# One-megabyte modulation units through GpSimd's queue, and recurrence results parked in DRAM, in a two-layer diffusion backbone

## The chip, the cores and the metric

The program runs on one core of a Trainium2 chip. The metric is the device time of one execution in microseconds (us); lower is better. A core has five engines with instruction streams of their own: TensorE (PE, matmuls), VectorE (DVE), ScalarE (ACT), GpSimd (POOL) and SyncE (SP, which here only issues transfers). Each engine takes its instructions strictly in order and waits on semaphores for the others. Transfers are issued from the streams of SP, ACT and POOL and run on 16 shared DMA engines.

## The reference

One inference step through two layers over 128 context and 256 latent tokens (384 columns in all) of width 2048. What matters here is the modulation (a linear map of the conditioning vectors, for each layer 2048 x 6144 weights, used as shift, scale and gate) and the first layer, where a recurrence and a Fourier mixer run as parallel head groups, each with a gate:

```python
m = (jax.nn.silu(cond) @ w + b)[..., None, :]      # modulation, split into shift, scale, gate
...
hp = _rmsnorm(xp, norm_pre[layer]) * (1.0 + sc_p) + sh_p
...
proj = h @ w_in
...
o, s_fin = _wkv_scan(...)                          # recurrence over the tokens, 16 heads of 64
o = ((o - mean) * lax.rsqrt(var + GN_EPS)).reshape(bsz, t_len, A_WIDTH)
o = o * gn_w.astype(f32) + gn_b.astype(f32)
y_a = (o + bonus.reshape(bsz, t_len, A_WIDTH)) * jax.nn.silu(gate_a)
y_b = y_b * jax.nn.silu(gate_b)
y = jnp.concatenate([y_a, y_b], axis=-1).astype(h.dtype) @ w_out
...
xp = xp + g_p * _rmsnorm(yp, norm_post[layer])
```

The second layer is grouped windowed attention with the same kind of modulation.

## The kernel before

**Weights.** All projections stream through `Stream` (L206): a raw tile of 256 KB (`raw<-we`, later `weo`, `wo`, `woo`) is loaded by SP (L236), ACT rounds it to a high part `whi` (L260), DVE subtracts to get `wlo` (L261), and PE forms three products for each block of activations (`mm3`), accumulating in `acc` (L404). In the recurrence the raw tiles have two buffers (`RAWB = 2`).

**Modulation.** The modulation weights are cut into blocks of 512 columns, and each block into four units of 1 MB (512 of the 2048 rows each, laid out as 128 partitions of 2048 numbers). The blocks are computed in four places. The blocks of layer 0's shift and scale run on PE in the head (`layer0_in`, tiles `mraw`, seven buffers). The blocks of `FILL_MODS` run on PE inside the recurrence (`fill_lane`, tile `rawf`). `PE_MODS` run on PE and `DVE_MODS` on DVE later, through `Stream` (tile `raw`). On PE, `mod_unit` multiplies a unit by the conditioning vectors in four matmuls that stand side by side in the array and accumulate in `ps_mod`. A trace shows each of these as two records, L406 for the first of a group and L410 for the rest. After a block's fourth unit ACT copies the sums to a row tile (`mrow`, L331), PE transposes it piece by piece (`ps_mt`), and DVE adds the bias (L338).

**The fill.** In the recurrence a unit is loaded in halves of 256 columns: 7 blocks x 2 halves x 4 = 56 loads of 512 KB into one buffer, each issued by SP as soon as the matmuls of the half before are done:

```python
raw = kp.tile([128, 4, 256], F32, name="rawf", tag="rawf", bufs=1)
w = self.mod_w(layer, b, u).rearrange("p (k c) -> p k c", k=4)
nc.sync.dma_start(raw, w[:, :, c0:c0 + 256])
```

**The recurrence.** Eight pairs of heads (j = 0 to 7) go through lanes that `weave` interleaves: the shifted projections (`proj_lane`), elementwise work (`wkv_elem`, with `ya`, the bonus term, at L1013), triangular systems (`wkv_lower`, and `wkv_solve` for two pairs together, whose long row of small DVE steps is L1118 and L1120), scores (`wkv_score`), the chain over chunks (`wkv_chain`) and the group norm (`wkv_norm`), which adds the normed output to `ya` (L1290). The `ya` tiles of all eight pairs (eight buffers) stay in SBUF until their gates are multiplied in (`make_y`, L540), after the recurrence and the Fourier part. GpSimd only clears small tiles here (`p` at L965, `SV` at L1172).

**What sets the order.** `weave` picks, by estimates written into the lanes, which lane emits its next piece, and so gives each instruction a priority. The fill lane's estimate for a piece is `FILL_PACE`. A list scheduler then sets the order on each engine by these priorities and by its own model of when operands are ready. Each engine, and each engine's queue of transfers, keeps that order at run time: a transfer that has to wait for its buffer holds up what stands behind it in the stream of its engine.

Of the kernel before, what the change touches and what calls it, by code (L numbers as in the profile page):

```python
# [11 lines left out]
F32 = mybir.dt.float32  # L12
# [10 lines left out]
T = TP + TS  # L23
# [4 lines left out]


FILL_MODS = [(0, 8), (0, 9), (0, 10), (0, 11), (1, 0), (1, 4), (1, 1)]  # L30
FILL_PACE = 5
PE_MODS = [(1, 5), (1, 2)]
DVE_MODS = [(1, 6), (1, 3), (1, 7)], [(1, 8), (1, 9), (1, 10), (1, 11)]

# [271 lines left out]
class K:  # L306
# [5 lines left out]
    def mod_unit(self, raw, layer, b, u, dst, c0=0):  # L312

        nc = self.nc
        key = layer, b, c0
        n = raw.shape[1] // 4
        if u == 0:  # L320
            self.macc[key] = self.pw.tile([128, 512], F32, name="ps_mod", tag="pw")
        acc = self.macc[key]
        with self.together():
            for i in range(4):
                kt = 4 * u + i
                self.mm(acc[32 * i:32 * i + 32, :n], self.silu[:, 2 * kt:2 * kt + 32], raw[:, n * i:n * i + n],
                                 start=(u == 0), stop=(u == 3), skip_group_check=True)
        if u < 3:
            return
        rows = self.mpool.tile([128, n], F32, name="mrow", tag="junk", bufs=1)  # L330
        nc.scalar.copy(rows, acc[:, :n])  # L331
        ps = self.pw.tile([128, 512], F32, name="ps_mt", tag="pw")
        m0, nm = c0 // 128, n // 128
        with self.together():
            for m in range(nm):
                self.mm(ps[:, 2 * m:2 * m + 2], rows[:, 128 * m:128 * m + 128], self.sel, start=True, stop=True)
        m1 = 48 * layer + 4 * b + m0
        nc.vector.tensor_tensor(dst[:, m0:m0 + nm], ps[:, 0:2 * nm].rearrange("p (m c) -> p m c", c=2),  # L338
                                self.modb[:, m1:m1 + nm].unsqueeze(2).to_broadcast([128, nm, 2]), op=ALU.add)
        del self.macc[key]  # L340
# [218 lines left out]
    def build(self):  # L559
# [4 lines left out]
        with ExitStack() as ctx:  # L564
            self.pw = ctx.enter_context(tc.tile_pool(name="pw", bufs=5, space=PSUM))
            self.pa = ctx.enter_context(tc.tile_pool(name="pa", bufs=3, space=PSUM))
            self.dp = ctx.enter_context(tc.tile_pool(name="dp", bufs=1, space=bass.MemoryType.DRAM))
            cp = self.cp = self.open("cp")
            self.rawp = self.open("wp")
            self.hp = self.open("hp")  # L570

            cm = cp.tile([128, 384], F32, name="cmat")
            nc.scalar.dma_start(cm, A["cmat"])
            self.ident, self.bd, self.mask = cm[:, 0:128], cm[:, 128:256], cm[:, 256:384]
            self.par_t = cp.tile([128, NPAR], F32, name="par")
            nc.scalar.dma_start(self.par_t, A["par"])

            cc = self.par_t[:, 0:32]
            th = cp.tile([128, 32], F32, name="cth")
            self.sel32 = cp.tile([128, 32], F32, name="sel")  # L580
            nc.scalar.dma_start(self.sel32, A["csel"])
            self.sel = self.sel32[:, 0:2]
            self.modb = cp.tile([128, 96], F32, name="modb")
            nc.scalar.dma_start(self.modb, A["modbc"])
            self.mcols = cp.tile([128, 16, 4, 2], F32, name="mcols")
            nc.scalar.activation(th, cc, AF.Tanh, scale=0.5)
            nc.vector.tensor_scalar(th, th, 0.5, 0.5, op0=ALU.mult, op1=ALU.add)
            self.silu = cp.tile([128, 64], F32, name="silu")
            nc.vector.memset(self.silu[:, 32:64], 0.0)
            nc.vector.tensor_tensor(self.silu[:, 0:32].rearrange("p (k c) -> p k c", c=2), th.rearrange("p (c k) -> p k c", c=2),  # L590
                                    cc.rearrange("p (c k) -> p k c", c=2), op=ALU.mult)
            eps = cp.tile([128, 3], F32, name="eps")
            nc.vector.memset(eps[:, 0:1], RMS_EPS)
            nc.vector.memset(eps[:, 1:2], GN_EPS)
            nc.vector.memset(eps[:, 2:3], 15 * math.log(2.0))
            self.eps = eps

            self.x1d = self.dp.tile([128, 3, D], F32, name="x1d")
            self.gd = self.dp.tile([2, 2, D], F32, name="gd")

            self.sd = self.dp.tile([4, 2, 128, 4], F32, name="sd")
            sq = th.rearrange("p (q c k) -> p q c k", q=4, c=2)
            nc.vector.tensor_copy(sq, self.silu[:, 0:32].rearrange("p (q k c) -> p q c k", q=4, c=2))
            nc.scalar.dma_start(self.sd.rearrange("q c p k -> p q c k"), sq)
            self.macc = {}
            self.ws = Stream(self, self.plan())
            ys = self.layer0_mix()
            acts = self.out_proj(0, ys)
            ys = self.layer1_mix(acts)
            self.out_proj(1, ys)  # L610
            for name in ("dpm", "yg", "gp", "yq", "cp"):
                self.close(name)
# [61 lines left out]
    def layer0_mix(self):  # L674
# [111 lines left out]

        def fill_lane():

            self.mpool = kp
            jobs = [(layer, b, self.mod_dst(layer, b), c0, u) for layer, b in FILL_MODS for c0 in (0, 256) for u in range(4)]  # L790

            def load(layer, b, dst, c0, u):
                raw = kp.tile([128, 4, 256], F32, name="rawf", tag="rawf", bufs=1)
                w = self.mod_w(layer, b, u).rearrange("p (k c) -> p k c", k=4)
                nc.sync.dma_start(raw, w[:, :, c0:c0 + 256])
                return raw.rearrange("p k c -> p (k c)")

            raw = load(*jobs[0])
            for n, (layer, b, dst, c0, u) in enumerate(jobs):
                yield 0.5, 0, FILL_PACE  # L800
                self.mod_unit(raw, layer, b, u, dst, c0)
                if n + 1 < len(jobs):
                    raw = load(*jobs[n + 1])

        self.weave(main_lane(), score_lane(), chain_lane(0), chain_lane(1), norm_lane(), elem_lane((0, 2, 3, 4, 5, 6, 7)), elem_lane((1,)), proj_lane(), fill_lane(),
                   lead=LEAD)
        self.close("kp")
        y = [st["y"] for st in sts]
        self.rawp = self.mpool = self.daccp = self.open("dpm", "right")
        self.srow = self.mpool.tile([128, 2, 512], F32, name="srow")  # L810
        for q in range(4):
# [7 lines left out]
            return self.yp.tile([128, T], F32, name=nm, tag="yt", bufs=self.YB)  # L819

        ys = [None] * 16
        fp = self.open("fp")
        ch = fp.tile([128, 321], F32, name="dft")
        nc.sync.dma_start(ch, A["cdft"])
# [5 lines left out]
        for g in range(4):  # L830
# [2 lines left out]
                    ys[2 * g + m] = self.make_y(fp, accs[m], y[2 * g + m])  # L833

            self.run(self.proj_cm(256, acts, ga_done))
        self.close("fp")
        self.close("bk")
        self.close("yp0")
        self.close("hp")
# [92 lines left out]
    def wkv_elem(self, j, st):  # L932
# [75 lines left out]
        STT(sq, sq, self.hrk[:, j:j + 1], r, op0=ALU.mult, op1=ALU.mult)  # L1008
        ps = self.pw.tile([128, 512], F32, name="ps_b", tag="pw")
        self.mm(ps[:, :T], self.bd, sq, start=True, stop=True)  # L1010
        y = st["y"] = self.yp0.tile([128, T], F32, name="ya", tag="ya", bufs=8)
        yield 0, 0.67, 0
        TT(y, ps[:, :T], v, op=ALU.mult)  # L1013

# [256 lines left out]
    def wkv_norm(self, j, st):  # L1271
# [16 lines left out]
        TT(o, o, s2, op=ALU.mult)  # L1288
        ACT(o, o, AF.Identity, scale=self.par("gw", j), bias=self.par("gb", j))
        TT(y, y, o, op=ALU.add)  # L1290


    def out_proj(self, layer, ys):
# [293 lines left out]
```

## Time and profile before

| | |
|---|---|
| runs before, us | 1600.28, 1600.47, 1605.43; median 1600.47 |
| profiled execution, us | 1596.4 |
| its span, first to last instruction, us | 1594.6 |
| PE busy in the span | 95% |
| mean granted TensorE clock, as a share of full speed | 0.984 |

The profiled execution is one run of its own: 1.8 us of its 1596.4 lie outside the span. By stage, in us from the start of the span: the head to about 130, the recurrence to about 705, the Fourier part and the gates to about 860, layer 0's output projection to about 1000, attention to about 1320, and the last gates with the output projection to the end. Busy times overlap, so that they say what an engine did, not what a stage waited for; the idle time before an instruction and what ended it says that.

### The profile page before, as it was taken

How to read it: one execution, taken by the hardware profiler on the slowest of the kernel's cores; microseconds unless marked ns; L12 is line 12 of the kernel's file. 1: busy time of each engine (PE TensorE's matmuls, PEld its weight loads, DVE VectorE, ACT ScalarE, POOL GpSimd, SP SyncE). 2: the span in 40 equal slices, each digit the busy share in tenths (PEclk: the TensorE clock that was granted, in tenths of full speed). 3: DMA queues.
4: the chain of work that ended last, by engine and by line, in shares of the span. 5: the costliest groups of instructions: out<-in, count | busy, mean ns of one | idle time of the engine just before them, and what ended most of it. 6: DMA issues, size and time to landing. Idle time of an engine off the chain costs nothing.

```text
span 1594.6 us, 30005 instructions
## 1 busy us (share of the span) xinstructions
PE 1507.3 (95%) x11488; PEld 1275.6 (80%) x11488; DVE 1069.1 (67%) x2584; ACT 810.9 (51%) x1771; POOL 3.9 (0%) x21
## 2 busy tenths in 40 slices
PE   7789999989998999999999998999999999999997
PEld 2557778767776778879998778988888889998777
DVE  1426896687777685574665755899878999653344
ACT  3326756857656655454333335744556555343332
POOL 0000000000000000000000000000000000000000
PEclk9899999999999999999999999899999999999999
DMA  9985352354333243444558664565322444447443
GB/s 365 375 311 164 123 160 78 102 167 122 97 107 110 86 143 90 132 152 126 174 189 325 211 207 144 200 225 204 100 73 73 133 132 140 125 122 242 125 120 139
DMA packets 120246, 255.74 MB, mean 160 GB/s; under 512 B 12324, under 2 KB 45220, under 8 KB 109732
## 3 DMA queue, kind: packets, MB, share of 16 engines
q1 hardware_dynamic: 111528, 235.97, 44.8%
q10 hardware_dynamic: 8576, 17.86, 3.2%
q8 instruction: 90, 1.47, 0.4%
q14 instruction: 52, 0.43, 0.1%
HBM read 246.40 MB, written 7.39 MB: 159 GB/s over the span
## 4 chain that ended last, share of the span: by engine, by line
PE 64%; DVE 16%; DMA 11%; ACT 6%; issue 3%; ACTq 0%; DVEq 0%; SPq 0%
PE acc L404 31%; PE acct L404 16%; DMA rawf<-modw 5%; DVE wlo L261 3%; PE ps_mod L406 3%; DVE junk L350 2%; DMA raw<-we 2%; DMA mraw<-modw 1%; DMA raw<-modw 1%; PE ps_o L410 1%; PE ps_v L410 1%; PE ps_pv L410 1%; ACT whi L260 1%; PE ps_s L410 1%; PE ps_sa L410 1%
## 5 line engine op out<-in xcount | busy, mean ns | idle before, releaser
L260 ACT CAST whi<-raw 128x512 fp32r<-128x512 f32 x480 | 295.5, 621 | 444.7 <-PE acc L404 196.5
L261 DVE TENSOR_TENSOR wlo<-raw,whi 128x512 fp32r<-128x512 f32 x480 | 327.5, 688 | 275.6 <-ACT whi L260 270.8
L404 PE MATMUL acc<-hhi,whi 128*128 128x384 f32 x1376 | 478.3, 348 | 12.5 <-ACT whi L260 5.7
L404 PE MATMUL acc<-hlo,whi 128*128 128x384 f32 x1376 | 472.9, 344 | 0.0
L404 PE MATMUL acc<-hhi,wlo 128*128 128x384 f32 x1376 | 470.7, 343 | 1.7 <-DVE wlo L261 1.3
L404 PEld LDWEIGHTS acc<-hhi,whi 128*128 128x128 f32 x1376 | 261.3, 190 | 44.2 <-issue 18.1
L404 PEld LDWEIGHTS acc<-hlo,whi 128*128 128x128 f32 x1376 | 261.3, 190 | 13.7 <-issue 11.9
L404 PEld LDWEIGHTS acc<-hhi,wlo 128*128 128x128 f32 x1376 | 260.9, 190 | 11.1 <-issue 5.5
L350 DVE SCALAR_TENSOR_TENSOR junk<-raw,srow 128x512 f32<-128x512 f32 x224 | 154.1, 688 | 8.6 <-DMA raw<-modw 5.2
L404 PE MATMUL acct<-whi,yhi 128*128 128x512 f32 (+1 forms) x432 | 154.4, 358 | 2.4 <-DVE yb L1318 2.1
L404 PE MATMUL acct<-wlo,yhi 128*128 128x512 f32 (+1 forms) x432 | 153.9, 356 | 0.0
L404 PE MATMUL acct<-whi,ylo 128*128 128x512 f32 (+1 forms) x432 | 153.7, 356 | 0.0
L404 PEld LDWEIGHTS acct<-whi,yhi 128*128 128x128 f32 x432 | 81.5, 189 | 20.7 <-DVE yb L1318 6.5
L404 PEld LDWEIGHTS acct<-whi,ylo 128*128 128x128 f32 x432 | 81.5, 189 | 12.4 <-issue 0.2
L404 PEld LDWEIGHTS acct<-wlo,yhi 128*128 128x128 f32 x432 | 81.5, 189 | 11.8
L406 PE MATMUL ps_mod<-rawf,silu 128*32 128x256 f32 x112 | 35.0, 395 | 22.5 <-DMA rawf<-modw 22.3
L406 PE MATMUL ps_mod<-mraw,silu 128*32 128x512 f32 x64 | 35.5, 668 | 9.7 <-DMA mraw<-modw 9.7
L1118 DVE TENSOR_TENSOR work<-work 128x30 f32<-128x30 f32 (+14 forms) x120 | 39.2, 327 | 2.1
L1120 DVE TENSOR_TENSOR work<-work 128x30 f32<-128x30 f32 (+14 forms) x120 | 39.2, 327 | 1.9
L1538 DVE TENSOR_REDUCE ast<-ps_sa 128x1 f32<-128x384 f32 x64 | 25.3, 415 | 20.3 <-PE ps_sa L410 20.1
L406 PEld LDWEIGHTS ps_mod<-rawf,silu 128*32 128x32 f32 x112 | 7.7, 108 | 36.2 <-DMA rawf<-modw 25.6
L410 PE MATMUL ps_mod<-rawf,silu 128*32 128x256 f32 x336 | 35.9, 395 | 0.0
(331 smaller groups left out, 2286.5 us busy)
## 6 DMA issues: line engine op xcount, KB each, us to landing
raw<-we SPq DMA_DIRECT2D x200, 256.0 KB, 2.9
raw<-wo SPq DMA_DIRECT2D x160, 256.0 KB, 2.7
raw<-modw SPq DMA_DIRECT2D x36, 1024.0 KB, 5.2
mraw<-modw SPq DMA_DIRECT2D x32, 1024.0 KB, 8.9
rawf<-modw SPq DMA_DIRECT2D x56, 512.0 KB, 3.9
raw<-weo SPq DMA_DIRECT2D x64, 256.0 KB, 2.9
raw<-woo SPq DMA_DIRECT2D x64, 256.0 KB, 2.7
G<-gd ACTq DMA_DIRECT2D x4, 1024.0 KB, 7.4
```

The lines of the kernel that those rows point to most:

```text
L260: k.nc.scalar.copy(hi, raw)
L261: k.nc.vector.tensor_tensor(lo, raw, hi, op=ALU.subtract)
L350: nc.vector.scalar_tensor_tensor(junk, raw[:, 512 * i:512 * i + 512], 1.0, self.srow[:, c], op0=ALU.mult, op1=ALU.mult, accum_out=self.dac ...
L404: op(*args, **kw)
L406: self.head.append(op(*args, **kw).ins)
L410: op(*args, **kw)
L1118: TT(tv, X[:, s + 1:32, s:s + 1].to_broadcast([128, n, s]), X[:, s:s + 1, 0:s].to_broadcast([128, n, s]), op=ALU.mult)
L1120: TT(X[:, s + 1:32, 0:s], X[:, s + 1:32, 0:s], tv, op=ALU.add)
L1538: nc.vector.tensor_reduce(st[:, 0, i:i + 1], src[i], axis=AX.X, op=ALU.max)
```

## The change

`fill_lane` loads whole units: 28 loads of 1 MB into one buffer `rawf` of twice the size, issued from GpSimd's stream, and `FILL_PACE` is doubled. `mod_unit` no longer has a row tile; the sums of a block are copied into the beginning of the raw tile of its last unit, whose buffer is then free only when the transposes have read it. This holds for all blocks that PE computes. The `ya` tiles have five buffers in place of eight: `wkv_norm` stores each finished result to DRAM (`yd`) from ACT's stream, and after the recurrence four buffers in a new pool `yl` bring them back through GpSimd's stream, four at once and two each after the first two gate blocks.

```diff
-FILL_PACE = 5
+FILL_PACE = 10
...
-        rows = self.mpool.tile([128, n], F32, name="mrow", tag="junk", bufs=1)
+        rows = raw[:, :n]
         nc.scalar.copy(rows, acc[:, :n])
...
+            self.yd = self.dp.tile([8, 128, T], F32, name="yd")
...
-            jobs = [(layer, b, self.mod_dst(layer, b), c0, u) for layer, b in FILL_MODS for c0 in (0, 256) for u in range(4)]
-
-            def load(layer, b, dst, c0, u):
-                raw = kp.tile([128, 4, 256], F32, name="rawf", tag="rawf", bufs=1)
-                w = self.mod_w(layer, b, u).rearrange("p (k c) -> p k c", k=4)
-                nc.sync.dma_start(raw, w[:, :, c0:c0 + 256])
-                return raw.rearrange("p k c -> p (k c)")
+            jobs = [(layer, b, u, self.mod_dst(layer, b)) for layer, b in FILL_MODS for u in range(4)]
+
+            def load(layer, b, u, dst):
+                raw = kp.tile([128, 2048], F32, name="rawf", tag="rawf", bufs=1)
+                nc.gpsimd.dma_start(raw, self.mod_w(layer, b, u))
+                return raw
...
-                yield 0.5, 0, FILL_PACE
-                self.mod_unit(raw, layer, b, u, dst, c0)
+                yield 1.0, 0, FILL_PACE
+                self.mod_unit(raw, *job)
...
+        yl = self.open("yl")
+        y = [None] * 8
+
+        def y_load(j):
+            y[j] = yl.tile([128, T], F32, name="y", tag="y", bufs=4)
+            nc.gpsimd.dma_start(y[j], self.yd[j])
+
+        for j in range(4):
+            y_load(j)
...
             self.run(self.proj_cm(256, acts, ga_done))
+            if g < 2:
+                y_load(2 * g + 4)
+                y_load(2 * g + 5)
...
-        y = st["y"] = self.yp0.tile([128, T], F32, name="ya", tag="ya", bufs=8)
+        y = st["y"] = self.yp0.tile([128, T], F32, name="ya", tag="ya", bufs=5)
...
         TT(y, y, o, op=ALU.add)
+        nc.scalar.dma_start(self.yd[j], y)
```

SP's stream early in the recurrence. Before (`raw` are projection weights, `rawf` the fill's halves):

```order
L795 DMA rawf_1191<-modw 128x4x256
L236 DMA raw_1105<-we 128x512
L236 DMA raw_1123<-we 128x512
L236 DMA raw_1146<-we 128x512
L795 DMA rawf_1310<-modw 128x4x256
L236 DMA raw_1164<-we 128x512
L236 DMA raw_1197<-we 128x512
L236 DMA raw_1223<-we 128x512
L236 DMA raw_1248<-we 128x512
L236 DMA raw_1266<-we 128x512
L795 DMA rawf_1341<-modw 128x4x256
L236 DMA raw_1347<-we 128x512
```

and with the change, from the end of the head to the end of the recurrence:

```order
L629 DMA mraw<-modw 128x2048
L236 DMA raw<-we 128x512 x120
L831 DMA dft<-cdft 128x321
L833 DMA dt<-cdt 128x646
L236 DMA raw<-modw 128x2048
```

The fill's loads have left SP, whose stream through the recurrence is now 120 weight loads in a row.

GpSimd's stream with the change, in the middle of the recurrence (`p` and `SV` are its memsets, which stood there alone before; `rawf_2966` is the load of unit 13, counted from 0):

```order
L794 DMA rawf_1947<-modw 128x2048
L794 DMA rawf_2070<-modw 128x2048
L794 DMA rawf_2281<-modw 128x2048
L976 MEMSET p_2741 128x12
L794 DMA rawf_2549<-modw 128x2048
L794 DMA rawf_2712<-modw 128x2048
L1183 MEMSET SV_3676 64x2x128
L1183 MEMSET SV_3678 64x2x128
L976 MEMSET p_3369 128x12
L794 DMA rawf_2966<-modw 128x2048
L794 DMA rawf_3020<-modw 128x2048
L794 DMA rawf_3123<-modw 128x2048
```

All 28 loads stand in GpSimd's stream between these memsets, and the eight `y<-yd` loads behind the last of them.

PE's stream at a place where two units of the fill follow closely, in the scores of a pair of heads (`ps_ba` is the triangular system, `ps_sc` the scores, `ps_bt` transposes). Before:

```order
L406 MATMUL ps_ba<-AR,BK 64x64
L410 MATMUL ps_ba<-AR,BK 64x64 x7
L406 MATMUL ps_sc<-AR,BK 128x128
L410 MATMUL ps_sc<-AR,BK 128x128 x7
L406 MATMUL ps_bt<-cmat,BK 128x128
L410 MATMUL ps_bt<-cmat,BK 128x128 x3
L406 MATMUL ps_bt<-cmat,BK 128x128
L410 MATMUL ps_bt<-cmat,BK 128x128
L406 MATMUL ps_mod<-rawf,silu 32x256
L410 MATMUL ps_mod<-rawf,silu 32x256 x3
L406 MATMUL ps_bt<-cmat,BK 128x128
L410 MATMUL ps_bt<-cmat,BK 128x128 x3
```

and with the change:

```order
L406 MATMUL ps_mod<-rawf,silu 32x512
L410 MATMUL ps_mod<-rawf,silu 32x512 x3
L406 MATMUL ps_ba<-AR,BK 64x64
L410 MATMUL ps_ba<-AR,BK 64x64 x15
L406 MATMUL ps_ba<-AR,BK 64x64
L410 MATMUL ps_ba<-AR,BK 64x64 x7
L406 MATMUL ps_sc<-AR,BK 128x128
L410 MATMUL ps_sc<-AR,BK 128x128 x7
L406 MATMUL ps_sc<-AR,BK 128x128
L410 MATMUL ps_sc<-AR,BK 128x128 x7
L406 MATMUL ps_mod<-rawf,silu 32x512
L410 MATMUL ps_mod<-rawf,silu 32x512 x3
```

A group of four matmuls now covers 512 columns, there are 28 groups in place of 56, and between the two shown here stand 24 `ps_ba` and 16 `ps_sc` matmuls. The work in between is otherwise that of before: in both programs 1728 projection matmuls stand ahead of the Fourier part's first.

## Rows read from the trace of the kernel before

**Rows 1.** The page's first lines: span, then busy time of each engine.
```profile
span 1594.6 us, 30005 instructions
PE 1507.3 (95%) x11488; PEld 1275.6 (80%) x11488; DVE 1069.1 (67%) x2584; ACT 810.9 (51%) x1771; POOL 3.9 (0%) x21
```
**Rows 2.** Stages: stretch, length, busy us of each engine, granted clock, DMA share, GB/s.
```profile
0.00:130.00 130.00, 105.44 (x580) 63.43 (x581) 38.50 (x77) 42.47 (x80) 1.29 (x9) 0.95 0.84 328
130.00:605.00 475.00, 441.68 (x4764) 356.81 (x4763) 362.73 (x911) 312.94 (x663) 2.57 (x12) 0.99 0.40 123
605.00:705.00 100.00, 95.16 (x1057) 83.84 (x1055) 58.72 (x135) 52.95 (x116) 0.00 (x0) 1.00 0.45 141
```
**Rows 3.** PE's waits from 130 to 605 us: us in total, times, longest.
```profile
PE ps_mod L406 <- DMA rawf<-modw: 22.3, 20, 4.8
PE ps_bt L406 <- DVE SC L1081: 2.3, 2, 2.0
```
**Rows 4.** PE in order of time, 422 to 427 us: start, us, instruction [idle before].
```profile
422.14 0.40 PE L406 MATMUL ps_mod<-rawf,silu 128*32 128x256 f32 x1 [0.41 <-DMA rawf<-modw]
...
422.71 0.44 PE L404 MATMUL acc<-hhi,whi 128*128 128x384 f32 x1
422.99 0.34 PE L404 MATMUL acc<-hlo,whi 128*128 128x384 f32 x1
423.16 0.35 PE L404 MATMUL acc<-hhi,wlo 128*128 128x384 f32 x1
...
426.13 0.34 PE L404 MATMUL acc<-hlo,whi 128*128 128x384 f32 x1
426.96 0.40 PE L406 MATMUL ps_mod<-rawf,silu 128*32 128x256 f32 x1 [0.49 <-DMA rawf<-modw]
```
**Rows 5.** The chain of waits at the same place: start, us, transfer.
```profile
422.84 4.08 DMA rawf<-modw
```
**Rows 6.** The tile `rawf`: count, ns min/median/max, first and last start.
```profile
L406 PE MATMUL ps_mod<-rawf,silu x112: 376/379/636, 135.9 to 600.8; 128*32 128x256 f32 x112
```
**Rows 7.** PE and SP in order of time, 480 to 492 us.
```profile
481.07 0.40 PE L406 MATMUL ps_mod<-rawf,silu 128*32 128x256 f32 x1
482.33 2.46 SPq L236 DMA_DIRECT2D raw<-we  x2
484.88 0.56 SPq L795 DMA_DIRECT2D rawf<-modw  x1
490.32 0.64 PE L406 MATMUL ps_mod<-rawf,silu 128*32 128x256 f32 x1 [4.77 <-DMA rawf<-modw]
```
**Rows 8.** PE at 771 us: a unit of 512 columns in a later stage.
```profile
771.28 0.34 PE L404 MATMUL acc<-hhi,wlo 128*128 128x384 f32 x1
771.55 0.62 PE L406 MATMUL ps_mod<-raw,silu 128*32 128x512 f32 x1
772.54 0.44 PE L404 MATMUL acc<-hhi,whi 128*128 128x384 f32 x1
772.82 0.34 PE L404 MATMUL acc<-hlo,whi 128*128 128x384 f32 x1
```
**Rows 9.** The page's transfers: count, KB each, median us from issue to landing.
```profile
raw<-modw SPq DMA_DIRECT2D x36, 1024.0 KB, 5.2
mraw<-modw SPq DMA_DIRECT2D x32, 1024.0 KB, 8.9
rawf<-modw SPq DMA_DIRECT2D x56, 512.0 KB, 3.9
```
**Rows 10.** PE from 319 to 321 us: first `ps_ba`, first `ps_sc` matmul.
```profile
319.64 0.27 PE L406 MATMUL ps_ba<-AR,BK 64*64 64x64 f32 x1
320.72 0.37 PE L406 MATMUL ps_sc<-AR,BK 64*128 64x128 f32 x1
```
**Rows 11.** DVE's copies from SBUF to SBUF, 130 to 605 us: busy us, mean ns.
```profile
L1253 DVE COPY work<-SV 64x256 f32<-64x256 f32 x12 | 3.5, 292 | 0.4
L1195 DVE COPY work<-SV 64x512 f32<-64x512 f32 x6 | 2.5, 425 | 8.7 <-ACT SV L1190 8.7
L1253 DVE COPY work<-SV 64x512 f32<-64x512 f32 x6 | 2.5, 424 | 2.9 <-ACT SV L1190 2.4 <-PE ps_o L410 0.6
```
**Rows 12.** GpSimd's waits in the whole span.
```profile
POOL p L965 <- DVE BK L1021: 200.7, 5, 67.7
```
**Rows 13.** DVE in order of time: pair 0's norm, then pair 5's `ya`.
```profile
311.24 0.55 DVE L1290 TENSOR_TENSOR ya<-ya,o 128x384 f32<-128x384 f32 x1
429.20 0.56 DVE L1013 TENSOR_TENSOR ya<-ps_b,v 128x384 f32<-128x384 f32 x1 [0.43 <-PE ps_b L404]
```
**Rows 14.** The tile `gth`: the gates' readings of `ya`.
```profile
L540 DVE SCALAR_TENSOR_TENSOR gth<-gth,ya x8: 551/551/554, 790.9 to 847.6; 128x384 f32<-128x384 f32 x8
```
**Rows 15.** The tile `SV`: a store that ACT issues in the recurrence.
```profile
L1244 ACTq DMA_DIRECT2D o_st<-SV x8: 564/598/628, 270.0 to 650.7; - x8
```

More of the change, by code (lines that the diff above doesn't have):

```diff
@@ L787, in fill_lane @@
         def fill_lane():
-            self.mpool = kp
-            jobs = [(layer, b, self.mod_dst(layer, b), c0, u) for layer, b in FILL_MODS for c0 in (0, 256) for u in range(4)]
-            def load(layer, b, dst, c0, u):
-                raw = kp.tile([128, 4, 256], F32, name="rawf", tag="rawf", bufs=1)
-                w = self.mod_w(layer, b, u).rearrange("p (k c) -> p k c", k=4)
-                nc.sync.dma_start(raw, w[:, :, c0:c0 + 256])
-                return raw.rearrange("p k c -> p (k c)")
+            jobs = [(layer, b, u, self.mod_dst(layer, b)) for layer, b in FILL_MODS for u in range(4)]
[3 more added lines that the diff above has]
+                return raw
             raw = load(*jobs[0])
-            for n, (layer, b, dst, c0, u) in enumerate(jobs):
-                yield 0.5, 0, FILL_PACE
-                self.mod_unit(raw, layer, b, u, dst, c0)
+            for n, job in enumerate(jobs):
+                yield 1.0, 0, FILL_PACE
+                self.mod_unit(raw, *job)
                 if n + 1 < len(jobs):
@@ L807, in layer0_mix @@
         self.close("kp")
-        y = [st["y"] for st in sts]
         self.rawp = self.mpool = self.daccp = self.open("dpm", "right")
@@ L835, in layer0_mix @@
             self.run(self.proj_cm(256, acts, ga_done))
+            if g < 2:
+                y_load(2 * g + 4)
+                y_load(2 * g + 5)
         self.close("fp")
+        self.close("yl")
         self.close("bk")
```

## The prediction

> **What bounds the kernel now.** Read the page's first lines [rows 1]: PE is busy 95% of the span, every other engine far less, so a change that leaves PE's work and waits alone is worth nothing. [...] PE's waits [rows 3] name the holes: 22.3 us in 20 waits end with the landing of a fill half, and the next entry has 2.3 us. Last, one such hole in order of time [rows 4, 5]: a half starts at 422.14, PE goes on with projections at 422.71, the reload of the single buffer is issued at 422.84, 0.70 us after the half began, and lands 4.08 us later; PE's other work ran out at about 426.5, so it stood 0.49 us. The rule to read from this: PE stands whenever less work lies between two units than a reload takes.
>
> **The fill's waits.** Let R be the time from PE's going on behind a unit to the next unit's landing: 0.13 us (422.84 less 422.71) plus the load. Before, R is about 4.2. Two of the 20 waits are of another kind: the longest, 4.77 us [rows 7], came because SP's stream stood on weight loads and issued the reload only at 484.88, 3.81 us after the unit, in place of 0.70. In GpSimd's stream no weight load stands ahead, so waits of this kind go; weight loads behind a waiting reload on SP get free too, which I cost at nothing since no wait of PE for weights comes near the first of [rows 3].
>
> For the new order I counted the PE work between each reload's release and the unit it feeds, at measured pitches: 0.17 us a projection matmul (422.99 to 423.16 [rows 4]), 0.067 us a `ps_ba` matmul (16 from 319.64 to 320.72 [rows 10]), about 0.12 us a `ps_sc` one, the others alike. The same count over the old order gives 328 us between the first and the last unit, where the trace has 600.8 - 135.9 = 465 us less 55 x 0.57 of units less 22.3 of waits, about 411 [rows 3, 4, 6]; small matmuls start slowly after a switch. I scale by 411/328 = 1.25. Of the 27 gaps of the new order ten are then below 7 us: 4.4, 4.4, 4.9, 5.0, 5.4, 5.4, 6.3, 6.4, 6.5 and 6.5, sum 55.2; the next is 7.6, all others 9.0 or more. In the gap behind a block's last unit the count starts at the transposes, because the row now lies in the raw buffer. The waits then come to 10R - 55.2, with R - 7.6 more once R passes 7.6.
>
> No row shows a load from GpSimd. The two rows of 1 MB [rows 9] bound it: 5.2 us from SP in the later stages, 8.9 us in the head, where seven loads stand in line and the DMA engines are 0.84 busy. The recurrence, at 0.40 [rows 2], is nearest to the first; I add 1.2 us, a third of the way, for a path that no row prices: load 6.4, R 6.5, waits 10.1 us. Against 22.3 that is **-12.2**; the ends are 2.6 us of waits (-19.7) and 36.2 (+13.9).
>
> [...]
>
> **The form of a unit.** A half holds PE from 422.14 to 422.71, 0.57 us, and the switch costs 0.10 us before it (771.28 to 771.55 in place of 0.17) and 0.11 behind it (422.71 to 422.99) [rows 4, 8]: 0.78. A unit of 512 columns runs from 771.55 to 772.54, 0.99 us, with the same two switches 1.20 [rows 8]. So 28 x (2 x 0.78 - 1.20) = **-10.1 us** of PE time. The transposes are as many as before.
>
> **What costs nothing, and its cover.** The memsets in GpSimd's stream: those of `p` waited up to 67.7 us for DVE before [rows 12], and a reload behind one waits along. In the new order only unit 13's reload stands behind such a memset with little PE work ahead (a gap of 5.0); the others have 10 us or more. Five `ya` buffers: pair 5 writes at 429.2, pair 0's norm is done at 311.8 [rows 13], over 110 us for the store. The eight stores cost ACT about 0.6 us each to issue [rows 15], 5 us on an engine that is busy 313 of 475 us [rows 2]. The loads back: four are issued long before the first gate at 790.9, and the last two, issued behind the second block of gates, have over 30 us to the last ones, near 845 [rows 14]. In the head a row kept in the raw buffer delays one of seven buffers, with a queue of loads ahead of it.
>
> **What is late next.** When PE runs ahead, it meets DVE (363 of 475 us busy) and ACT sooner in the long chains of solve and norm; the reordered program can place new waits. I take **+5 us**, between 0 (the 11 us of PE's other idle time stay) and 10 (they double).
>
> Sum: -12.2 - 10.1 + 5 = -17.3; 1596.4, the profiled execution's own time, becomes 1579.1. The median of the runs shown, 1600.47, is 4.1 above that execution, so on the scale of such runs I forecast 1583.2. Its own range is 1575 to 1592 (loads from 5.4 to 7.1 us and 0 to 10 for the rest). No change means within 0.3%, 4.8 us.
>
> **Rivals.**
> Loads as quick as SP's (5.2 us): waits fall to 2.6 us, -19.7 - 10.1 + 5 = -24.8, 1575.7. For it: the DMA engines have room [rows 2]. Against it: nothing shows GpSimd issuing as fast. Chance 0.15. [...]
>
> Given back inside the recurrence: the waits fall, but the recurrence's own chain through DVE and ACT sets the end, and PE waits for them in place of the fill; about 17 us in place of 5 come back further on, so that the time stays near 1596 to 1603, say 1600. For it: DVE is 76% busy in this stage. Against it: waits for DVE are 2.3 us at most per kind [rows 3], and the 100 us without fill run at 95% [rows 2]. Chance 0.20.
>
> Slower: GpSimd's loads take as long as the head's, 8.9 us. Then ten close pairs of units each stand 2.5 to 4.6 us, waits are 36.2, and +13.9 - 10.1 + 5 = +8.8 gives 1609.3. It turns to a loss from waits of 27.4 us on (22.3 + 10.1 - 5), R 8.2, a load of 8.1 us; beyond 8.5 it is over 0.3%. For it: one buffer, and a stream that prepares its transfers between memsets that wait. Against it: the 5.2 us row. Chance 0.17. [...]
>
> That the change does not do what it says is excluded for its form: the order shows 28 loads in GpSimd's stream, none on SP's, and the same projection work.
>
> **How the numbers follow.** Forecast 0.48 and quick loads 0.15 make 0.63 for faster; given back is 0.20 for the same; slower 0.17. The range runs from 1570 (quick loads and nothing given back) to 1607 (loads of about 8.6 us), and leaves out the far end of the slower case.
>
> **What would show it.** Right: 28 `rawf` loads with a median near 6.4 us; PE's waits for them near 10 us in about ten waits; units of about 1 us; PE's other waits in the recurrence hardly grown; the Fourier part starting some 17 us earlier, and nothing moved behind it; no wait of the gates for `y`. Wrong: a median above 8 us or waits above 27 us (slower); waits near 10 us but the Fourier part no earlier (given back); or a loss behind 705 us, from the stores or loads of `yd`.

## The result, and the profile after

The changed kernel takes 1616.29 us (median of 4 runs, 1613.73 to 1620.64), the kernel before beside it on the same chip 1600.79: a ratio of 1.0090, 95% interval [1.0066, 1.0113]. It is slower by about 15 us where 17 us of gain were forecast, and lies outside the range. The profiled execution took 1614.67 us.

The page's first lines and, by stretch, the same columns as [rows 2], of the changed kernel:

```profile
span 1612.8 us, 29536 instructions
PE 1515.9 (94%) x11264; PEld 1280.4 (79%) x11264; DVE 1069.0 (66%) x2577; ACT 807.7 (50%) x1764; POOL 23.2 (1%) x57
```
```profile
130.00:605.00 475.00, 440.78 (x4547) 356.67 (x4547) 357.36 (x891) 309.52 (x656) 17.46 (x40) 0.97 0.38 123
605.00:705.00 100.00, 92.86 (x1010) 81.38 (x1009) 58.03 (x132) 46.99 (x107) 1.60 (x3) 0.93 0.43 130
705.00:860.00 155.00, 154.64 (x907) 144.16 (x910) 99.66 (x235) 62.40 (x130) 2.15 (x4) 1.00 0.53 170
860.00:1000.00 140.00, 133.86 (x746) 110.94 (x739) 76.42 (x164) 49.52 (x97) 0.00 (x0) 0.98 0.62 209
```

PE has less to do (11264 matmuls in place of 11488) and is busy 9 us longer: the granted clock is 0.97 and 0.93 where [rows 2] have 0.99 and 1.00. PE's waits in the recurrence, 126 to 704 us, longest groups first:

```profile
PE ps_mod L406 <- DMA rawf<-modw: 5.0, 5, 1.6
PE ps_z L406 <- ACT work L1150: 4.6, 4, 2.0
PE acc L404 <- DVE wlo L261: 4.3, 3, 3.6
PE ps_m L404 <- ACT s L1292: 4.2, 4, 2.9
PE ps_b L404 <- DVE sq L1019: 3.9, 1, 3.9
PE ps_n L404 <- ACT work L967: 3.5, 1, 3.5
PE acc L404 <- ACT whi L260: 3.2, 2, 3.0
```

The fill's waits fell from 22.3 us [rows 3] to 5.0, but what [rows 3] show as 2.3 us at most per kind is now 3 to 5 us six times over, in single waits of up to 3.9 (in the same stretch of the kernel before, no kind but the fill has more than 2.9). One of them in order of time, PE from 246 to 261 us, and the granted clock there (columns as in [rows 2]):

```profile
246.10 0.59 PE L406 MATMUL ps_mod<-rawf,silu 128*32 128x512 f32 x1
...
250.59 1.62 PE L404 MATMUL ps_b<-sq,cmat 128*128 128x384 f32 x2 [3.88 <-DVE sq L1019]
...
258.74 0.52 PE L404 MATMUL acc<-hhi,wlo 128*128 128x384 f32 x1
259.06 0.52 PE L404 MATMUL acc<-hhi,whi 128*128 128x384 f32 x1
```
```profile
245.00:250.00 5.00, 1.72 (x54) 0.77 (x47) 5.00 (x16) 3.90 (x9) 0.53 (x1) 0.93 0.37 87
250.00:255.00 5.00, 3.92 (x48) 2.31 (x50) 4.36 (x10) 4.52 (x8) 0.12 (x1) 0.50 0.67 259
255.00:260.00 5.00, 5.00 (x73) 4.10 (x69) 2.74 (x9) 2.26 (x6) 0.00 (x0) 0.54 0.23 56
260.00:265.00 5.00, 5.00 (x49) 3.27 (x49) 1.55 (x4) 3.16 (x7) 0.00 (x0) 1.00 0.00 0
```

PE stood for 3.88 us and then ran until about 260 us at a granted clock of 0.50 (half clock): projection matmuls follow at 0.32 us (258.74 to 259.06) in place of 0.17 [rows 4]. By these two pitches the time in which PE has work in this stretch of 10.2 us loses about half its length; that is an estimate.

The transfers that the change adds, from the page and from the tiles `rawf`, `y` and `gth`:

```profile
rawf<-modw POOLq DMA_DIRECT2D x28, 1024.0 KB, 5.3
```
```profile
DMA to landing us min/median/max: 5.0/5.3/8.4
```
```profile
L540 DVE SCALAR_TENSOR_TENSOR gth<-gth,y x8: 549/551/554, 799.2 to 856.1; 128x384 f32<-128x384 f32 x8
```

The second loss is in layer 0's output projection. DVE, in order, at 874 us:

```profile
874.52 0.69 DVE L261 TENSOR_TENSOR wlo<-raw,whi 128x512 fp32r<-128x512 f32 x1
887.50 0.69 DVE L350 SCALAR_TENSOR_TENSOR junk<-raw,srow 128x512 f32<-128x512 f32 x1 [12.28 <-DMA raw<-modw]
```
and PE:
```profile
889.66 0.79 PE L404 MATMUL acct<-wlo,yhi 128*128 128x512 f32 x1 [6.14 <-DVE wlo L261]
```

DVE stands 12.28 us for a `raw<-modw` of DVE's own modulation blocks, the next `wlo` stands behind it in DVE's stream, and PE waits 6.14 us for that `wlo`; a half-clock stretch of 6.8 us begins in that wait. In the kernel before, DVE's waits for `raw<-modw` in this stage are 1.8 us at most, and PE waits for no `wlo`.

To compare kernels stage by stage, every trace is cut at the same work: the recurrence runs from the start of the 201st to that of the 1701st matmul on `acc` or `acct`, the output projection from the 2401st to the 2801st. In the recurrence the table gives PE's idle time, the part of it that a fill load ended ("fill") and that DVE or ACT ended ("chain"), and the time at half clock; what is left after idle time and half of the half-clock time is PE's work at full clock.

| kernel | length | idle | fill | chain | half clock | work |
|---|---|---|---|---|---|---|
| before | 569.7 | 37.1 | 22.5 | 14.6 | 13.7 | 525.7 |
| after | 577.7 | 41.4 | 5.1 | 36.3 | 44.4 | 514.1 |
| e7, order as before | 571.4 | 31.7 | 17.4 | 14.2 | 30.7 | 524.3 |
| e3, halves, row in the raw tile | 579.5 | 36.3 | 20.1 | 16.2 | 37.5 | 524.4 |
| e16, halves, pace 4 | 599.5 | 50.9 | 20.6 | 30.2 | 47.8 | 524.7 |
| e1, halves on GpSimd | 576.7 | 40.4 | 19.4 | 21.0 | 20.5 | 526.0 |
| e8, order as after | 588.1 | 47.3 | 5.9 | 41.5 | 51.2 | 515.2 |
| e12, e9 on GpSimd | 579.9, 581.6 | 44.5, 42.7 | 3.7, 1.3 | 40.8, 41.5 | 30.7, 47.8 | 520.1, 515.0 |
| e4 on GpSimd, pace 16 | 566.3 | 34.4 | 0 | 34.4 | 37.5 | 513.1 |
| e10, e13 on SP | 569.8, 570.9 | 33.5, 32.3 | 2.7, 3.4 | 30.7, 28.8 | 37.5, 47.8 | 517.6, 514.8 |
| e14, e15 on SP | 568.9, 564.3 | 35.1, 30.5 | 3.8, 0.4 | 31.3, 30.1 | 30.7, 30.7 | 518.5, 518.4 |
| e17, e18 on SP | 587.8, 566.1 | 47.7, 33.3 | 9.5, 3.7 | 38.2, 29.6 | 44.4, 30.7 | 517.9, 517.4 |
| e11, no fill | 543.7 | 42.3 | 0 | 42.3 | 37.5 | 482.7 |

One execution of one order scatters: in the recurrence e7 has the order of instructions of the kernel before on every engine, and e8 that of after, and they differ by 2 and 10 us from them. So groups are compared, not single lines. Two of e4's 28 units run behind this stretch.

### The profile page after: what moved, and what is told of

Its sections match the earlier page's. It is cut to its first block, busy times and chain, and to the rows that moved or that the text cites. A ratio compares the mean times of both kernels' runs of the same rounds, so it can differ in the third digit from the quotient of the medians.

```text
span 1612.8 us, 29536 instructions
## 1 busy us (share of the span) xinstructions
PE 1515.9 (94%) x11264; PEld 1280.4 (79%) x11264; DVE 1069.0 (66%) x2577; ACT 807.7 (50%) x1764; POOL 23.2 (1%) x57
## 4 chain that ended last, share of the span: by engine, by line
PE 62%; DVE 17%; ACT 9%; DMA 8%; issue 3%; ACTq 0%; DVEq 0%; SPq 0%; POOLq 0%
PE acc L404 29%; PE acct L404 16%; DMA raw<-we 4%; DVE wlo L261 3%; DVE junk L350 2%; PE ps_mod L406 2%; DMA rawf<-modw 1%; ACT whi L260 1%; DMA raw<-modw 1%; PE ps_v L410 1%; PE ps_o L410 1%; PE ps_pv L410 1%; PE ps_s L410 1%; DVE work L1131 1%; DVE work L1129 1%
## 5 line engine op out<-in xcount | busy, mean ns | idle before, releaser
L404 PE MATMUL acc<-hhi,whi 128*128 128x384 f32 x1376 | 481.4, 350 | 13.0 <-ACT whi L260 11.6
L350 DVE SCALAR_TENSOR_TENSOR junk<-raw,srow 128x512 f32<-128x512 f32 x224 | 154.2, 689 | 19.8 <-DMA raw<-modw 16.4
L406 PE MATMUL ps_mod<-mraw,silu 128*32 128x512 f32 x64 | 37.2, 689 | 13.0 <-DMA mraw<-modw 13.0
L1550 DVE TENSOR_REDUCE ast<-ps_sa 128x1 f32<-128x384 f32 x64 | 25.4, 417 | 20.1 <-PE ps_sa L410 20.1
L410 PE MATMUL ps_mod<-mraw,silu 128*32 128x512 f32 x192 | 37.5, 690 | 0.0
L406 PE MATMUL ps_mod<-rawf,silu 128*32 128x512 f32 x56 | 31.0, 637 | 5.1 <-DMA rawf<-modw 5.0
L1201 ACT COPY SV<-ps_v 64x512 f32<-64x512 f32 (+1 forms) x32 | 15.2, 475 | 40.0 <-PE ps_v L410 35.1
```

Of the source, the lines that this page charges most:

```text
L350: nc.vector.scalar_tensor_tensor(junk, raw[:, 512 * i:512 * i + 512], 1.0, self.srow[:, c], op0=ALU.mult, op1=ALU.mult, accum_out=self.dac ...
L404: op(*args, **kw)
L406: self.head.append(op(*args, **kw).ins)
L410: op(*args, **kw)
L1201: nc.scalar.copy(SV[64:128, :, 0:ns, :], pv)
L1550: nc.vector.tensor_reduce(st[:, 0, i:i + 1], src[i], axis=AX.X, op=ALU.max)
```

## Experiments

The theories: **used up early** (units served faster leave PE nothing to put into the chain's waits later), **held buffer** (the row in the raw tile), **GpSimd's queue**, and **order** (the list scheduler's new order is worse by luck). The pace, `FILL_PACE`, sets how far apart the planner puts the units. Ratios are to the kernel before on the same chip, with 95% intervals.

**One part of the change at a time, on the kernel before.**

e1, the halves from GpSimd's queue:
```diff
-                nc.sync.dma_start(raw, w[:, :, c0:c0 + 256])
+                nc.gpsimd.dma_start(raw, w[:, :, c0:c0 + 256])
```


> The kernel before, with the fill's 56 halves issued from GpSimd's stream and nothing else changed. Theory 'used up early' (28 whole units are served faster, so the fill is used up at 507 us in place of 600, and PE then meets the solve and norm chains of DVE and ACT in fewer but longer waits, each followed by a stretch at the lower clock): halves and pace are those of before, the fill still ends near 600 us, time within 0.4% of before; the one 4.77 us wait behind SP's weight loads is gone. Theory 'order' (any rebuild shuffles the list schedule, and the loss is the luck of one order): the order hardly changes here, also within 0.4%. Theory 'GpSimd's loads are dear': slower, waits for the fill above the 22.3 us of before.

Measured 1606.88, ratio 1.0046 [1.0025, 1.0066]. It is slower, as the third theory had it, but not for its reason: the loads landed after 3.8 us, as from SP [rows 9], the fill's waits fell to 19.4 us, and yet the chain's waits grew from 14.6 to 21.0. The order changed with the queue: about 140 of PE's 5792 matmuls in the recurrence stand elsewhere.

e2, the `yd` trip of the change alone (its lines on `yd`, `yl`, `y_load` and five `ya` buffers):

> The kernel before, with only the recurrence's results stored to DRAM and read back (five ya buffers, stores from ACT, loads from GpSimd). 'Used up early': within 0.4% of before, half-clock time in the recurrence near the 14 us of before. 'Stores': if ACT's eight waiting stores are what delays the chains, at least half of the 8 us lost in the recurrence shows here, and the DFT starts 4 us or more later. 'Order': anything within 1%, either sign.

Measured 1603.5, 1.0022 [1.0003, 1.0041]; no stage shows where those 3 us would be (recurrence 569.0), so this stays open.

e3, the row in the raw tile everywhere:
```diff
-        rows = self.mpool.tile([128, n], F32, name="mrow", tag="junk", bufs=1)
+        rows = raw[:, :n]
```


> The kernel before, with only the row of sums kept in the raw tile. 'Used up early': within 0.4% in the recurrence. For the second loss, 8 us in layer 0's output projection: if the row that holds a raw buffer until its transposes is the cause, DVE's wait of 12 us for a modulation load and the 8 us show here too; if not, the output projection takes as long as before (140 us from 860 to 1000).

Measured 1615.3, 1.0103 [1.0068, 1.0139]. The row alone, with halves on SP, loses as much as the whole change. Its recurrence takes 579.5 us against 569.7, more than the 0.4% that "used up early" allowed, and its output projection 108.3 against 101.0. To see which row costs, e5, e6 and e7 do it in Stream (stage 2 in the line below), in the fill (stage 1) and in the head (stage 0) alone:

```diff
+        rows = raw[:, :n] if self.stage in (2,) else self.mpool.tile([128, n], F32, name="mrow", tag="junk", bufs=1)
```


> The kernel before, with one part of the change in one place: the sums of the two PE_MODS blocks that go through Stream are copied into their raw tile; in the head and in the recurrence's fill they keep a row tile of their own. Theory held buffer: the row keeps one of Stream's two 1 MB buffers until the transposes, and the planner puts two 1 MB loads and the DVE work on them next to each other, so DVE waits 6 to 12 us for raw<-modw near 875 us, a wlo stands behind it and PE with it: layer 0's output projection grows by 7 to 8 us (from 101 to about 108), the recurrence stays at 569.7 within 2, total about 1607 to 1609. Rival, order by luck: the loss appears only together with the other rows, and this kernel stands at 1600 within 3, with 101 to 104 us in the projection.

> The kernel before, with the row in the raw buffer only in the recurrence's fill; head and Stream keep a row tile. Theory held buffer: behind a block's last half the single buffer now waits for ACT's copy and PE's transposes, 14 times, and PE's fill waits get longer and fewer, with stretches at half granted clock behind them: the recurrence grows by about 8 to 10 us as in the run with the row everywhere (579.5), the output projection stays at 101 to 104, total about 1608 to 1611. Rival, order by luck: the recurrence's growth does not come with the fill's row, and it stays at 569 to 573; total 1600 to 1604.

> The kernel before, with the row in the raw buffer only in the head, where seven buffers stand; fill and Stream keep a row tile. By the prediction this costs nothing in the head (124.9 within 1). A control for order by luck: DVE's order in the recurrence changes although nothing there is changed. If luck of the list order is worth several us, the recurrence leaves 569.7 by over 3 us either way; if the loss is tied to what a row holds up, it stays within 3 and the total at 1600 within 3.

e5: 1606.88, 1.0045 [1.0019, 1.0071], recurrence 568.6, output projection 109.5 against 101.0 before and 104.6 in e7. PE's and DVE's waits in e5's output projection:
```profile
PE acct L404 <- DVE wlo L261: 6.8, 2, 6.2
```
```profile
DVE junk L350 <- DMA raw<-modw: 12.8, 2, 7.6
```
e6: 1604.82, 1.0032 [1.0012, 1.0053], recurrence 574.3, projection 104.3. e7: 1600.79, 1.0012 [0.9994, 1.0030]. The row in Stream's two buffers is a held buffer. The row in the fill costs about half of what was expected of it, and how stays open: the fill's waits are as before, 21.3 us against 22.5, and the order changed (about 200 of PE's matmuls stand elsewhere). In the head the row is free. As a control for luck e7 says little, since DVE's order in the recurrence came out as before, not changed as was expected.

**The changed kernel, one thing undone.** e4 has FILL_PACE 16; e8 has the row in the raw tile only in the fill; e9 and e12 are e8 with FILL_PACE 13 and 12.

> The changed kernel with the fill's pace at 16 in place of 10, so that its 28 units are spread as far as the 56 halves were (the last near 600 us). 'Used up early': the recurrence is back to before or better, DFT from 695 to 706 us in place of 713.8, half-clock time there 14 to 25 us in place of 44, the whole 1598 to 1608. 'Order': no tie between the fill's end and the time; as likely slower than faster, 1590 to 1625. 'Stores or row': stays at 1610 to 1620.

> The changed kernel, with the row in the raw buffer only in the fill (where a row tile does not fit beside the 1 MB buffer); head and Stream keep a row tile of their own. Theory held buffer: the wait of DVE for raw<-modw near 875 goes and the output projection comes back from 109.1 to 101 to 104, total 1608 to 1611. Rival, the projection's loss belongs to the y loads or to the later start of the G<-gd loads: it stays at 108 to 109 and the total near 1616. The recurrence is expected at 577 within 4 by both.

> The changed kernel with a row tile of its own in head and Stream, as in the run before this one, and FILL_PACE 13 in place of 10, which puts the last unit behind 1459 projection matmuls of the recurrence in place of 1200 (before: 1392). Theory used up early: with units left for longer, PE's waits for DVE and ACT in the last third are filled, half-clock time falls, and the recurrence comes to 566 to 572 with the Fourier part at 150 and the output projection at 104: total 1595 to 1601. Rival, the chain through DVE and ACT has its price wherever the units stand, or the order is worse by itself: recurrence 576 to 588 as with pace 10, total 1608 to 1614.

> As the pace 13 kernel, with FILL_PACE 12: the last unit behind 1284 projection matmuls. Theory used up early: between pace 10 and pace 13, recurrence 570 to 580, total 1599 to 1609. Rival, luck of the order: no trend with pace, this one is as likely below the pace 13 kernel as above it.

e4: 1619.78, 1.0123 [1.0089, 1.0158]. Its recurrence came back to 566.3, as "used up early" had it, but the chain's waits stayed at 34.4; the last units run in the Fourier part, which takes 168.8 us in place of 149.0. e8: 1613.49, 1.0096 [1.0064, 1.0128]: the projection came back from 109.1 to 103.7 as the held buffer says, but the total not measurably; the recurrence of the traced execution, expected at 577 within 4, took 588.1. e9: 1615.48, 1.0063 [1.0038, 1.0087]; e12: 1612.44, 1.0057 [1.0038, 1.0076]: the last unit came at 617 and 577 us in place of 508, and the chain's waits stayed at 41. "Used up early" falls: units that last longer don't fill the chain's waits.

e11 leaves the fill out:

> The changed kernel without the fill: the seven FILL_MODS blocks are neither loaded nor computed, their columns are cleared on GpSimd, so the output lacks them. It measures what the fill costs PE. If PE is the bound of the recurrence, as the prediction took it, the 28 units' 1.2 us each and their waits come off: 577.7 - 34 - 5 = 539 or less. If the chain through DVE and ACT is the bound, PE's waits for them grow by most of what is taken away and the recurrence stays at 555 to 575. In between both share it.

Measured 1578.14; the recurrence is 543.7, 34 us shorter than after, near the 539 of a PE-bound stage. PE's work is the bound. With no fill at all the chain's waits are 42.3 us, and PE's idle time is no shorter than before the change, when a fill load ended most of it.

**Whole units on SP.** e10 is the changed kernel with one word changed; e13, e14 and e15 are e8, e12 and e9 with it.
```diff
-                nc.gpsimd.dma_start(raw, self.mod_w(layer, b, u))
+                nc.sync.dma_start(raw, self.mod_w(layer, b, u))
```


> The changed kernel with the 28 whole units issued from SP's stream in place of GpSimd's. If GpSimd's queue has a part in the loss (descriptors, memsets ahead of a load), the fill's waits stay near 5 and the recurrence gets shorter by over 5 us. By the theory that the loss comes from the chain through DVE and ACT, the queue makes no difference but for reloads that stand behind weight loads: fill waits 3 to 12, waits for DVE and ACT near 36, the recurrence 574 to 588, the output projection still 108 to 110, total 1612 to 1620.

> Whole units from SP's stream, row tile of its own in head and Stream, FILL_PACE 10; the twin on GpSimd is the run with the row in the fill alone (1613.5). Its recurrence has the order of the run with whole units on SP and the row everywhere (569.8 there). Theory GpSimd's queue: 8 to 10 us below its twin, 1602 to 1606, with the output projection at 104. Theory luck of the order: the difference to the twin is 0 within 4.

> As the run before it with FILL_PACE 12; the twin on GpSimd stands at 1612.4. Theory GpSimd's queue: again 6 to 10 us below its twin, 1602 to 1607, whatever the order. Theory luck of the order: no fixed sign, 1600 to 1620.

> As the run before it with FILL_PACE 13; the twin on GpSimd stands at 1615.5. Theory GpSimd's queue: 6 to 10 us below its twin, 1605 to 1610. Theory luck of the order: no fixed sign, 1600 to 1620.

| | on GpSimd | on SP |
|---|---|---|
| change as it is (after, e10) | 1616.29, 1.0090 | 1606.02, 1.0016 [0.9994, 1.0038] |
| row in the fill alone (e8, e13) | 1613.49, 1.0096 | 1603.95, 1.0023 [1.0002, 1.0043] |
| and pace 12 (e12, e14) | 1612.44, 1.0057 | 1596.34, 0.9986 [0.9972, 1.0000] |
| and pace 13 (e9, e15) | 1615.48, 1.0063 | 1602.57, 1.0022 [0.9999, 1.0044] |
| halves (e1, before) | 1606.88, 1.0046 | 1 |

Each line is a pair of twins, which differ in the queue. In five pairs of five GpSimd is slower, by 0.4 to 0.7%. In e10 the first theory held (the recurrence is 7.9 us shorter than after), though no run shows the descriptors that it names as a cause, and the second, 1612 to 1620, missed; e13 came where GpSimd's queue had it, e14 and e15 below their ranges. In the four pairs with whole units ACT also waits longer for projection weights. In the recurrence, after and then e13:
```profile
ACT whi L260 <- DMA raw<-we: 56.8, 33, 8.1
```
```profile
ACT whi L260 <- DMA raw<-we: 45.1, 33, 8.3
```
It is 41.9 to 45.6 us in the four kernels with whole units on SP and 52.0 to 70.5 in the four on GpSimd. In the fifth pair it hardly grows, from 38.8 to 40.6. The loads that ACT waits for aren't slower, though: the median weight load takes 2.7 us in all eight, as here in after and then in e10, from 130 to 700 us:
```profile
raw<-we SPq DMA_DIRECT2D x130, 256.0 KB, 2.7
```
```profile
raw<-we SPq DMA_DIRECT2D x132, 256.0 KB, 2.7
```
Weight loads in flight together with a fill load, where the trace has both landings, take 3.4 to 3.7 us on average in the four on GpSimd and 3.4 to 3.9 in the four on SP. And ACT's wait is 49.4 us in e11, where there is no fill load to collide with. So these waits don't show a collision in the twins.

**The queue, with the order held.** The twins differ in their order of instructions too: 140 to 200 of PE's matmuls in the recurrence stand elsewhere. e17 and e18 are e14 with 16 transfers on GpSimd's queue that nothing waits for; between these two the order is the same on every engine.
```diff
+            self.nc.gpsimd.dma_start(self.xd[self.xn][:, :2048], self.A["modw"][self.xn][:, :2048])
```
(`:16` in e18)

> Whole units on SP at FILL_PACE 12 (1596.3), plus 16 transfers of 1 MB from DRAM to DRAM on GpSimd's queue, one behind each memset of p and SV, that nothing waits for. Theory GpSimd's queue gets in the way on the chip: ACT's waits for raw<-we grow from 44.8 towards 60 to 70 and the time by 5 to 12 us, to 1601 to 1608. Rival, the order of instructions makes the difference between the twins: 1596 within 3, with ACT's waits for raw<-we within 5 of the other run of this call.

> The same with 8 KB in place of 1 MB each, in the same order of instructions: GpSimd's work of issuing without the bytes. If issuing from GpSimd costs by itself, this one is as slow as the run with 1 MB; if the bytes cost, it stays at 1596 within 3 while the other is slower; by the rival both stay at 1596 within 3.

e17: 1613.14, 1.0070 [1.0045, 1.0096]; e18: 1596.76, 0.9969 [0.9948, 0.9990]. Issuing costs nothing that shows; the bytes of 16 transfers of 1 MB beside SP's loads cost 16.4 us. The longest of the delayed loads in e17's chain of waits, PE's waits for ACT's rounding (126 to 255 us), and the same load in e18, issued at 126.05 (the transfers issued from 126 to 126.2 us):
```profile
127.15 10.47 DMA raw<-we
```
```profile
PE acc L409 <- ACT whi L260: 6.3, 3, 5.9
```
```profile
raw<-we SPq DMA_DIRECT2D x1, 256.0 KB, 2.7
```
Three transfers of 1 MB had been issued at 124.5, 125.3 and 126.7; a 256 KB weight load issued behind them on another queue took 10.47 us where it takes 2.7 in e18, and PE stood 5.9 us where the longest such wait in e18 is 0.6. But ACT's waits for `raw<-we` grew only from 51.6 us in e18 to 54.7, not towards 60 to 70, and e18 has 51.6 and is as fast as e14 with 44.8: that sum doesn't tell a slow kernel from a fast one. What grew in e17's recurrence is in the table: the fill's waits by 5.8 us, the chain's by 8.6, half-clock time by 13.7 (the traced execution of e17 is its slowest). e17 moves 16 MB more than e14, from DRAM to DRAM, so it shows that such a collision is possible and its price, not that the twins' difference is one.

e16, the kernel before with FILL_PACE 4:

> The kernel before, halves on SP, with FILL_PACE 4 in place of 5: its last half stands behind 1261 projection matmuls of the recurrence (1392 before, 1200 with the change). Theory used up early: waits for DVE and ACT in the last third grow, and the kernel is 5 to 10 us slower than before, 1606 to 1611. Rival: the halves come more densely, fill waits grow by 3 to 6 us and nothing else changes, 1602 to 1606; or the order changes nothing, 1600 within 3.

Measured 1620.44, 1.0121 [1.0096, 1.0146]: a miss by all theories, some 20 us for one unit of pace. Fill waits stayed (20.6), chain waits doubled to 30.2 and 47.8 us ran at half clock. The order that the pace gives is worth more than any term of the sum, and it can double the chain's waits without any fill wait taken away.

## Why the prediction was wrong

In the recurrence, in the sum's own terms (after less before in the table): PE's work fell by 11.6 us (forecast 10.1) and the fill's waits by 17.4 (forecast 12.2), but the waits for DVE and ACT grew by 21.7 (forecast 5), and 30.7 us more at half clock cost about half of that by the pitches above (0.32 us in place of 0.17), 15.4, for which the sum had no term. Together that is 8.0 us more where 17.3 less were forecast. The output projection, taken as unchanged, added 8.1. The line of the kernel before is a good execution (e7, in the same order, has 30.7 us at half clock and 104.6 in the projection), so part of the last two sizes is scatter.

**The fill's waits: the mechanism was right, the gain larger than forecast.** Loads were taken as 6.4 us and waits as 10.1; they were 5.3 (the shortest of the 28 took 5.0), and 5.0 in five waits. The 0.13 us did not hold: from GpSimd most reloads are issued 0.40 us after PE goes on, from SP 0.13. The count of PE work between units did: with R = 0.40 + 5.3 = 5.7 the six shortest gaps give 4.7 us of waits. The count's factor of 1.25 was put down to small matmuls that start slowly after a switch: in the trace of before the first `ps_ba` matmul of [rows 10] starts 0.27 us behind the last projection matmul (319.37 to 319.64), where those are 0.17 apart, and the second 0.11 behind the first, where the 16 average 0.067; that this makes up the whole factor was the author's estimate.

**The form of a unit: right.** PE's work was 524 to 526 us with halves and is 513 to 520 with whole units, where the sum had 10.1 less.

**"What is late next": the step that failed.** It was +5, between 0 and 10, argued from [rows 3], where DVE and ACT cost 2.3 us at most per kind; over all kinds they cost 14.6 us in the recurrence. Those rows were taken while PE also stood 22 us for the fill. With whole units on SP the chain's waits went from about 15 to about 30: of some 18 us of fill waits removed, 15 came back. With whole units on GpSimd they are 34 to 42, and with no fill at all 42. The rival "given back inside the recurrence" had this, and nearly the size. The likely reason is that the holes gave DVE and ACT time to come first; that is argued, not shown, since every one of these kernels also has a new order, and e16's order alone doubled the chain's waits. On top comes the clock. In after all six waits of 2 us or more in the recurrence are for DVE or ACT, and each has a half-clock stretch beside it; the kernel before has two such waits, one of them with a stretch, and its 20 fill waits are 1.1 us on average. Half-clock time is 13.7 and 30.7 us in the two executions with the order of before, 44.4 and 51.2 with that of after. No term held a clock.

**The queue was priced for its own loads alone.** The prediction asked how long a load from GpSimd takes, and put down as free that "weight loads behind a waiting reload on SP get free too". By the twins the move to GpSimd, with the order that comes with it, costs 0.4 to 0.7%, 7 to 12 us. What in it costs is not shown: in e17 1 MB transfers on another queue held up a weight load (10.47 us where it takes 2.7 in e18), but the twins' weight loads are as quick on either side. The rival that made it slower had the sign, and by the twins the place, GpSimd's queue; its mechanism was wrong, since the loads took 5.3 us, not 8.9, and the fill's waits fell.

**The row.** The prediction put a row in the fill into its count of gaps, took one in the head as free, and did not look at Stream, whose two buffers have DVE waiting behind them in order. In the head it is free; in the fill, with halves, it costs 0.3% (e6); in Stream the output projection takes 106.5 to 109.5 us with it and 101.0 to 106.4 without.

**The rest.** Memsets behind waiting reloads: no engine waited for GpSimd. The gates did not wait for `y`: from 704 to 853 us is 149.0 us, before 150.1. The median load from GpSimd is 0.2 to 0.4 us longer than from SP in the four pairs with whole units, and nothing here tells why. The loss behind 705 us that was to speak for `yd` came from the row: e5 has it without `yd`, and e8 has `yd` without it.

What stays open: whether the twins' difference is the queue itself or the order that comes with it, how much of the chain's growth is order, what the row in the fill holds up, and the 3 us of e2. One test is missing: the same order on every engine, with the queue alone changed.

## What to carry to other kernels

A wait that goes from the profile's list may have been time in which other engines caught up: before taking it off the sum, ask what the bound engine would meet next if it came there earlier, add up all kinds of its other waits and not the largest alone, and count a stop of several us twice where the trace has a half-clock stretch beside stops of that length (an estimate from after: its six waits of 2 us or more come to 19.0 us, and half of the 34.1 us at half clock beside them is 17.1). Before giving a large load a queue of its own, look at who waits for the small, urgent loads on the other queues. Where a planner sets the order, measure first what a change of order alone is worth, as e16 does. The same edit with the load left on SP, the row kept out of Stream and pace 12 (e14) is level with the kernel before, 0.9986 [0.9972, 1.0000], and the best that was found.

## What the runs showed of the hardware

The median load of 1 MB takes 5.2 to 5.3 us from GpSimd and 4.8 to 5.0 from SP in the same stage, and from GpSimd most are issued 0.40 us after PE goes on, from SP 0.13. Issuing 16 transfers of 8 KB from GpSimd cost nothing that shows, 16 of 1 MB from DRAM to DRAM 16.4 us. In after, each of the recurrence's eight half-clock stretches begins within 2 us of the end of a wait of 1.5 to 3.9 us, and they last 3.4 to 10.2 us; one in e8, at a wait of 4.5 us, lasts 20.5. In an execution with the same order as before (e7) 17 us more at half clock went with 5 us less idle time and only 1.7 us more length: if half of the 17 us is what the lower clock cost, most of it came off the waits.
